# Where the final rows are stored: two output tensors shaped like the result, or one whose rows follow the partitions

## The chip, the cores and the metric

The kernel runs on one core of a Trainium2 chip. The metric is the device time of one launch in microseconds (us). Work that numpy does on the host before or behind the launch is not in it; the joining of output pieces that this case speaks of is such work.

A core has five engines that matter here: PE (matrix products), DVE (element-wise work), ACT (element-wise functions), POOL (small copies and sums) and SP, which computes nothing and issues most of the transfers. A transfer (DMA) is issued by one instruction of SP's queue, and then carried out by the core's 16 DMA engines as packets; here a packet is one run of contiguous bytes, 2 KB in the final stores.

## The reference, cut to what matters

One layer of a streaming encoder is computed for two groups of requests that share the weights: 256 new rows of a prompt and 32 rows of a running sample, each row 2048 numbers wide.

```
xn   = rmsnorm(x, norm_mix_pre);  proj = xn @ w_in
mix  = concat[pool(proj), ssd(proj)] @ w_out
x    = x + rmsnorm(mix, norm_mix_post)
hn   = rmsnorm(x, norm_ffn_pre);  up = conv3(hn @ w_up)
f    = (silu(up[:, :5632]) * up[:, 5632:]) @ w_down
y    = x + rmsnorm(f, norm_ffn_post)      # y_prompt (1, 256, 2048), y_sample (1, 32, 2048)
```

Beside the two `y`, eight histories and states are returned. Everything is float32.

## The kernel before

**Layout.** The 288 rows (256 prompt, 32 sample) stand along the free axis of every tile, and the features along the 128 partitions. A matrix product takes a 128x128 block of a weight and a 128x288 tile of activations. Each float32 operand is split into a rounded part and a rest (`whi`, `wlo`; lines 130 and 131), and each block is multiplied three times (lines 136 to 138). The weights come in by 1 MB transfers that SP issues (`raw`, line 115).

**Order.** A scheduler sets each engine's order from the program, except where the code pins instructions. At the end of the program much is pinned by hand.

**The end of the program.** The down projection gives 16 tiles `part` of 128 features x 288 rows. The result is wanted by rows, so each tile is turned: fourteen of them through DVE's block transpose and a scratch tensor `fd` in DRAM (function `to_tokens`), the last two by PE with an identity (function `turn`). After that a row's features stand along the free axis, in pieces of 512 columns:

- `ft[2*q + b]` is 128 x 512: rows 128*b to 128*b+127 of the prompt, columns 512*q to 512*q+511. There are eight of them, and eight tiles `xr` of the same form, which hold the residual `x`.
- `ft_s` and `xr_s` are 128 x 512 too, but for the sample: with 32 rows only, partition 32*q + s holds row s and columns 512*q to 512*q+511.

What is left is `xr = ft * rf + xr` on DVE (`rf` is the inverse root mean square of each row) and the store. The function `y_out(q, b)` does this for one piece of the prompt and stores it by line 962; the sample's piece is computed in line 1030 and stored by line 1032. The order is: four pieces with b = 1 (their rows are finished first), the sample's piece, then PE's last sums, `rf` for the first 128 rows, and four pieces with b = 0. All nine stores are issued by SP, each 256 KB in 128 runs of 2 KB. Behind them stands the end of the program (line 1105), where SP waits for every DMA semaphore and then all engines meet.

The nine stores in the code:

```python
sp.dma_start(out=y_prompt[0][b * P : (b + 1) * P, 512 * q : 512 * (q + 1)], in_=x)   # line 962, eight times
sp.dma_start(out=y_sample[0].rearrange("s (q c) -> q s c", q=4), in_=xr_s)           # line 1032, once
```

The first store's destination is a pattern of 128 rows x 512 columns with a step of 8 KB from row to row. The second one's is a pattern of three levels: 4 (q) x 32 (s) x 512 (c); q steps by 2 KB and s by 8 KB. On the side of the tile both are 128 partitions x 512 columns.

Of the kernel before, what the change touches and what calls it, by code (L numbers as in the profile page):

```python
# [16 lines left out]
P = 128  # L17
TC = {"schedule_with_timeline_sim": True}
D_MODEL = 2048
NP_ = 256  # L20
NS = 32
NT = NP_ + NS
D_POOL = 1024
D_SSD = 2048
# [6 lines left out]
NF = D_FF // P  # L31
NXC = CONV // P
NU = D_POOL // P
# [10 lines left out]
def body(  # L44
# [14 lines left out]
    w_up2,  # L59
    w_up,  # L60
    w_down,
    y_prompt,
    y_sample,
    new_pool,
    new_sconv,
    new_ssd_p,
# [4 lines left out]
    act, dve, pool, pe, sp = nc.scalar, nc.vector, nc.gpsimd, nc.tensor, nc.sync  # L71
# [97 lines left out]
    def blocks_out(d, t, src, pool_):  # L169
# [17 lines left out]
        out=tri, in_=tri, pattern=[[1, P]], compare_op=ALU.is_ge, fill=0.0, base=0, channel_multiplier=-1  # L187
# [62 lines left out]
    for kb, n in chunks:  # L250
# [12 lines left out]
        for k in range(kb, kb + n):  # L263
# [14 lines left out]
            for m in range(6):  # L278
                c = slice(m * P, (m + 1) * P)
# [75 lines left out]
    def htile(name, n=NT, tag=None):  # L355
        return mp.tile([HEADS, n], F32, tag=tag or name, name=name, bufs={"z": 4}.get(tag, 2) if tag else 1)
# [22 lines left out]
    r = htile("r", tag="z")  # L379
# [295 lines left out]
    for gi in range(2):  # L675
        c = slice(gi * P, (gi + 1) * P)
# [85 lines left out]
    for k in range(KD):  # L762
# [14 lines left out]
        else:  # L777
            q = op_.tile([P, NT], F32, tag="sq", bufs=2, name="sq")
# [11 lines left out]
        for m in range(7):  # L790
            c = slice(m * P, (m + 1) * P)
# [33 lines left out]
    f = []  # L825
# [56 lines left out]
    xr_s = apool.tile([P, 512], F32, tag="a", name="xr_s")  # L882
# [68 lines left out]
    def y_out(q, b):  # L951

        x = xr[2 * q + b]
        f_ = ft[2 * q + b]
        for o, n, src in (
            ((0, 512, f_),) if q < 3 else ((0, 2 * P, f_[:, : 2 * P]), (2 * P, 2 * P, last[b]))
        ):
            c = slice(o, o + n)
            ins = dve.scalar_tensor_tensor(x[:, c], src, rf[:, b : b + 1], x[:, c], op0=ALU.mult, op1=ALU.add)  # L959
            if b:  # L960
                tc.keep_in_program_order(ins)
        sp.dma_start(out=y_prompt[0][b * P : (b + 1) * P, 512 * q : 512 * (q + 1)], in_=x)

    n_tok = [0]

# [20 lines left out]
    for kb, n in ((0, K_RUN), (K_RUN, 8), (K_RUN + 8, 8)):  # L986
# [4 lines left out]
        for piece in split_w(raw, kb, n, 256):  # L991
            for low in (True, False) if kb else (True,):
                for j in range(2):
                    c = slice(j * P, (j + 1) * P)
# [16 lines left out]
    for j in range(2):  # L1011
        c = slice(j * P, (j + 1) * P)
        for i, (k, hi, lo) in enumerate(held):
            tc.keep_in_program_order(
                pe.matmul(pb[j], hi[:, c], f2[k][:, :, B], start=k == K_RUN, stop=k == HALF - 1)
            )
            if j == 0 and i == 13:
                for i in range(2):
                    feature_sums(fsq[i], 0, False, i == 1)
                final_rstd(0)  # L1020
            if j == 1 and i == 2:
                for i in range(2):
                    turn(i, 0)
                act.activation(ft_s[P - NS :, 2 * P :], last[2][P - NS :, :], AF.Copy)
        if j:
            for q in range(4):
                y_out(q, 1)
        run_out(j, 1, pb[j], fsq[j])
    tc.keep_in_program_order(
        dve.scalar_tensor_tensor(xr_s, ft_s, rf[:, 2:3], xr_s, op0=ALU.mult, op1=ALU.add)  # L1030
    )
    sp.dma_start(out=y_sample[0].rearrange("s (q c) -> q s c", q=4), in_=xr_s)
    p_f.append(acc_ps.tile([P, 4], F32, tag="acc", name="psum_f"))
    last[0] = acc_ps.tile([P, 2 * P], F32, tag="acc", name="pft")
    feature_sums(fsum, 1, True, False)
# [5 lines left out]
    for q in range(4):  # L1041
        y_out(q, 0)
# [1 line left out]


_OUTS = [
    (1, 256, 2048), (1, 32, 2048), (P, 2, 15, NU), (P, 2, 3, NXC), (P, D_SSD), (P, D_SSD), (P, 2, 2, 2 * NF),
]


# [70 lines left out]
```

## Time and profile before

| | |
|---|---|
| median of 3 runs | 1338.72 us (1338.0 to 1338.82) |
| the profiled execution's own time | 1337.7 us |
| its span, first to last instruction | 1336.0 us |
| PE busy | 1312.7 us, 98% of the span |
| DVE, ACT, POOL busy | 887.1, 665.3, 239.8 us |
| share of the 16 DMA engines taken by SP's queue | 55.4% |
| moved by DMA | 249.82 MB |

A row of the profile names the line of the code, the engine, the operation and the tiles as out<-in, then count and times. `SPq` is SP's queue: the instruction that issues a transfer, not the transfer itself. In the profile every output tensor is called `out`, so `out<-xr` is one of the eight stores of the prompt's pieces and `out<-xr_s` that of the sample's piece. For transfers a list gives the time from issue to landing, that is, to the semaphore that says that all of it has arrived. In a table by stretches of time, "DMA share" is the mean busy share of the 16 DMA engines, so one engine alone gives 0.06.

### The profile page before, as it was taken

Reading aid. Unit: us, or ns where it says so; the run is one execution under the profiler, and the core shown is the slowest. Engines: PE = TensorE matmul, PEld = TensorE weight load, DVE = VectorE, ACT = ScalarE, POOL = GpSimd, SP = SyncE. Lnnn points to the kernel's source line nnn. Section 1 sums busy time; section 2 is a strip of 40 time slices with the busy share of each in tenths; the row PEclk is TensorE's granted clock in tenths of the full one; section 3 lists DMA queues with packets and bytes.
Section 4 is the critical chain, followed back from the end, with each engine's and each line's share of the span. In section 5 each row is a group of like instructions: output and inputs, shape, how many; then the busy total and the mean of one; then the engine's idle time right before and its main releaser. Section 6 shows DMA issues by size and latency. Waiting matters only on the chain.

```text
span 1336.0 us, 25101 instructions
## 1 busy us (share of the span) xinstructions
PE 1312.7 (98%) x10041; PEld 1297.0 (97%) x10041; DVE 887.1 (66%) x1437; ACT 665.3 (50%) x1002; POOL 239.8 (18%) x376
## 2 busy tenths in 40 slices
PE   7999999999999999999999999999999999999996
PEld 7999999999999989999999999999999999999996
DVE  7898998788544469977676644335666666664444
ACT  7558777446443455644445433334454444454442
POOL 6221102240212123211121100001111111101110
PEclk9999999999999999999999999999999999999998
DMA  7667884456656435766544544554544544566653
GB/s 285 230 194 258 280 248 150 152 207 216 238 205 205 146 121 189 208 180 187 179 158 164 176 146 170 174 182 159 181 166 158 174 174 158 168 239 175 208 177 94
DMA packets 104009, 249.82 MB, mean 187 GB/s; under 512 B 63748, under 2 KB 69444, under 8 KB 81492
## 3 DMA queue, kind: packets, MB, share of 16 engines
q1 hardware_dynamic: 101972, 243.11, 55.4%
q0 software_dynamic: 1488, 4.92, 1.1%
q8 instruction: 78, 1.28, 0.4%
q14 instruction: 39, 0.32, 0.1%
q10 hardware_dynamic: 432, 0.19, 0.1%
HBM read 236.23 MB, written 11.95 MB: 186 GB/s over the span
## 4 chain that ended last, share of the span: by engine, by line
PE 91%; DVE 3%; DMA 2%; issue 1%; POOL 1%; ACT 0%; SPq 0%; DVEq 0%; POOLq 0%; ACTq 0%
PE acc L138 30%; PE acc L136 29%; PE acc L137 29%; DMA xw<-xs_d 1%; POOL xs L640 1%; DMA raw<-in_w_first 1%; DVE xn L100 1%; PE py L467 1%; DMA xs_d<-blocks 1%; DVE wlo L271 0%; DVE xr L959 0%; PE acc_x L138 0%; PE run_a L1002 0%; PE acc_x L137 0%; DVE wlo L131 0%
## 5 line engine op out<-in xcount | busy, mean ns | idle before, releaser
L131 DVE TENSOR_TENSOR wlo<-raw,whi 128x1024 fp32r<-128x1024 f32 (+1 forms) x386 | 464.3, 1204 | 329.4 <-ACT whi L130 328.7
L130 ACT ACTIVATE whi<-raw 128x1024 fp32r<-128x1024 f32 (+1 forms) x386 | 399.3, 1036 | 471.9 <-PE acc L137 384.9
L138 PE MATMUL acc<-hn,wlo 128*128 128x288 f32 x1376 | 409.3, 298 | 0.0
L136 PE MATMUL acc<-hn,whi 128*128 128x288 f32 x1376 | 402.5, 293 | 0.5 <-ACT hn L770 0.5
L137 PE MATMUL acc<-hn,whi 128*128 128x288 f32 x1376 | 399.6, 291 | 1.2 <-DVE hn L771 1.2
L137 PEld LDWEIGHTS acc<-hn,whi 128*128 128x128 f32 x1376 | 258.9, 188 | 1.5 <-DVE hn L771 1.4
L136 PEld LDWEIGHTS acc<-hn,whi 128*128 128x128 f32 x1376 | 258.7, 188 | 1.3 <-ACT hn L770 1.3
L138 PEld LDWEIGHTS acc<-hn,wlo 128*128 128x128 f32 x1376 | 258.7, 188 | 0.0
L136 PE MATMUL acc<-xn,whi 128*128 128x288 f32 x688 | 203.8, 298 | 5.6 <-ACT whi L270 5.6
L137 PE MATMUL acc<-xn,whi 128*128 128x288 f32 x688 | 200.8, 293 | 0.0
L138 PE MATMUL acc<-xn,wlo 128*128 128x288 f32 x688 | 198.7, 298 | 1.6 <-DVE wlo L271 1.4
L138 PE MATMUL acc<-fa,wlo 128*128 128x288 f32 x660 | 196.4, 298 | 0.0
L136 PE MATMUL acc<-fa,whi 128*128 128x288 f32 x660 | 193.1, 293 | 0.0
L137 PE MATMUL acc<-fa,whi 128*128 128x288 f32 x660 | 191.4, 290 | 0.0
L136 PEld LDWEIGHTS acc<-xn,whi 128*128 128x128 f32 x688 | 130.3, 189 | 6.5 <-ACT whi L270 5.6
L137 PEld LDWEIGHTS acc<-xn,whi 128*128 128x128 f32 x688 | 130.3, 189 | 0.2
L138 PEld LDWEIGHTS acc<-xn,wlo 128*128 128x128 f32 x688 | 127.7, 189 | 2.6 <-DVE wlo L271 1.6
L137 PEld LDWEIGHTS acc<-fa,whi 128*128 128x128 f32 x660 | 123.9, 188 | 0.0
L136 PEld LDWEIGHTS acc<-fa,whi 128*128 128x128 f32 x660 | 123.9, 188 | 0.0
L138 PEld LDWEIGHTS acc<-fa,wlo 128*128 128x128 f32 x660 | 123.9, 188 | 0.0
L816 POOL COPY fc_stage<-ebuf 128x4 f32<-128x4 f32 x88 | 27.2, 309 | 466.8 <-DVE ebuf L815 466.8
L812 POOL COPY ebuf<-pf 128x2 f32<-128x2 f32 x88 | 67.4, 767 | 140.6 <-DVE fc L822 79.4
(279 smaller groups left out, 1716.1 us busy)
## 6 DMA issues: line engine op xcount, KB each, us to landing
raw<-in_w_up SPq DMA_DIRECT2D x80, 1024.0 KB, 4.8
raw<-in_w_in SPq DMA_DIRECT2D x38, 1024.0 KB, 5.4
raw<-in_w_down SPq DMA_DIRECT2D x32, 1024.0 KB, 4.8
raw<-in_w_out SPq DMA_DIRECT2D x24, 1024.0 KB, 4.8
raw<-in_w_down SPq DMA_DIRECT2D x16, 768.0 KB, 4.3
raw<-in_w_up SPq DMA_DIRECT2D x8, 896.0 KB, 4.5
gb<-g_d SPq DMA_DIRECT2D x8, 832.0 KB, 6.6
raw<-in_w_first SPq DMA_DIRECT2D x7, 768.0 KB, 10.2
```

What stands on the lines that cost most here:

```text
L100: dve.scalar_tensor_tensor(a[:, 1, :], src, scale, a[:, 0, :].bitcast(F32), op0=ALU.mult, op1=ALU.subtract),
L130: act.activation(hi, raw[:, k : k + n, :], AF.Copy)
L131: dve.tensor_tensor(lo, raw[:, k : k + n, :], hi.bitcast(F32), op=ALU.subtract)
L136: pe.matmul(out, wh, a[:, 0, :], start=start, stop=False)
L137: pe.matmul(out, wh, a[:, 1, :], start=False, stop=False)
L138: pe.matmul(out, wl, a[:, 0, :], start=False, stop=stop)
L467: pe.matmul(y[:, 0:256], xw[:, 0, c], m[:, j, 0:256], start=True, stop=False)
L640: pool.tensor_tensor(xs[t], xs[t], rg[1], op=ALU.mult)
L812: pool.tensor_copy(e[:, 258:260], pf[:, 4:6, i])
L816: pool.tensor_copy(fc_stage[:, :, :, i], e[:, 256:324].rearrange("p (s c) -> p s c", c=34)[:, :, 0:2])
```

## The change

The two output tensors `y_prompt` (1, 256, 2048) and `y_sample` (1, 32, 2048) become one tensor `y_rows` of 128 x 9 x 512. Its first axis is the partition. Piece 4*b + q of the prompt goes to `y_rows[:, 4*b + q, :]` and the sample's piece to `y_rows[:, 8, :]`, exactly as they stand in the tiles. The step from row to row in DRAM is now 9 x 2 KB = 18 KB for all nine stores, and the pattern of each has two levels, 128 x 512. Behind the launch numpy reorders the pieces into the two results.

```diff
-    y_prompt,
-    y_sample,
+    y_rows,
...
-        sp.dma_start(out=y_prompt[0][b * P : (b + 1) * P, 512 * q : 512 * (q + 1)], in_=x)
+        sp.dma_start(out=y_rows[:, 4 * b + q, :], in_=x)
...
-    sp.dma_start(out=y_sample[0].rearrange("s (q c) -> q s c", q=4), in_=xr_s)
+    sp.dma_start(out=y_rows[:, 8, :], in_=xr_s)
...
 _OUTS = [
-    (1, 256, 2048), (1, 32, 2048), (P, 2, 15, NU), (P, 2, 3, NXC), (P, D_SSD), (P, D_SSD), (P, 2, 2, 2 * NF),
+    (P, 9, 512), (P, 2, 15, NU), (P, 2, 3, NXC), (P, D_SSD), (P, D_SSD), (P, 2, 2, 2 * NF),
 ]
...
+    y_p = _np.ascontiguousarray(y[:, :8].reshape(P, 2, D_MODEL).transpose(1, 0, 2)).reshape(1, NP_, D_MODEL)
+    y_s = _np.ascontiguousarray(y[:, 8].reshape(4, NS, 512).transpose(1, 0, 2)).reshape(1, NS, D_MODEL)
```

The end of SP's queue before the change, with what each instruction waits for (a semaphore of DVE, or one of the eight DMA semaphores `DMAHW` that the stores take in turn):

```order
L904 DMA ft_s<-fd 32x256
L962 DMA out<-xr 128x512 [waits DVE_49] x4
L1032 DMA out<-xr_s 4x32x512 [waits DVE_49]
L962 DMA out<-xr 128x512 [waits DMAHW3_49,DVE_49]
L962 DMA out<-xr 128x512 [waits DMAHW4_49,DVE_49]
L962 DMA out<-xr 128x512 [waits DMAHW5_49,DVE_49]
L962 DMA out<-xr 128x512 [waits DMAHW6_49,DVE_49]
L1105 UNCONDITIONAL_BRANCH
```

And the same place of SP's queue after it:

```order
L903 DMA ft_s<-fd 32x256
L961 DMA out<-xr 128x512 [waits DVE_49] x4
L1031 DMA out<-xr_s 128x512 [waits DVE_49]
L961 DMA out<-xr 128x512 [waits DMAHW3_49,DVE_49]
L961 DMA out<-xr 128x512 [waits DMAHW4_49,DVE_49]
L961 DMA out<-xr 128x512 [waits DMAHW5_49,DVE_49]
L961 DMA out<-xr 128x512 [waits DMAHW6_49,DVE_49]
L1104 UNCONDITIONAL_BRANCH
```

Nothing has moved: the lines count one less, the waits are the same, and the one row that reads otherwise is the sample's store, 128x512 in place of 4x32x512. On PE, DVE, ACT and POOL every instruction stands in the same order as before.

More of the change, by code (lines that the diff above doesn't have):

```diff
@@ L1107 @@
     r = _run(nc, [arrays], core_ids=[0])
-    y_p, y_s, n_pool, n_sconv, h_p, h_s, n_fconv = (_np.asarray(r.results[0][f"out_{i}"]) for i in range(len(_OUTS)))
+    y, n_pool, n_sconv, h_p, h_s, n_fconv = (_np.asarray(r.results[0][f"out_{i}"]) for i in range(len(_OUTS)))
     def rows(a, s):
```

## The prediction

> **What bounds the kernel now.** I began with the page's first part and its chain of work, to see whether the end of the program is worth looking at.
>
> ```profile
> span 1336.0 us, 25101 instructions
> PE 1312.7 (98%) x10041; PEld 1297.0 (97%) x10041; DVE 887.1 (66%) x1437; ACT 665.3 (50%) x1002; POOL 239.8 (18%) x376
> ```
>
> PE works for 98% of the span. The change touches none of its instructions and none of its inputs, so what happens before the last product is the same. What counts is how long the core goes on after PE. I read that from the order of time at the end: first DVE and PE's last rows, then SP's queue, both from the view by time.
>
> ```profile
> 1321.85 2.47 DVE L959 SCALAR_TENSOR_TENSOR xr<-ft,rf,xr 128x512 f32<-128x512 f32 x4
> 1324.24 0.48 DVE L959 SCALAR_TENSOR_TENSOR xr<-pft,rf,xr 128x256 f32<-128x256 f32 x1
> 1325.21 0.74 DVE L1030 SCALAR_TENSOR_TENSOR xr_s<-ft_s,rf,xr_s 128x512 f32<-128x512 f32 x1
> 1326.12 0.33 PE L913 MATMUL pft<-ident,part 128*128 128x128 f32 x1
> 1326.60 2.47 DVE L959 SCALAR_TENSOR_TENSOR xr<-ft,rf,xr 128x512 f32<-128x512 f32 x4
> 1328.99 0.48 DVE L959 SCALAR_TENSOR_TENSOR xr<-pft,rf,xr 128x256 f32<-128x256 f32 x1
> ...
> 1322.62 2.45 SPq L962 DMA_DIRECT2D out<-xr  x4
> 1325.98 0.68 SPq L1032 DMA_DIRECT2D out<-xr_s  x1
> 1327.38 4.13 SPq L962 DMA_DIRECT2D out<-xr  x4
> ```
>
> PE is done at 1326.45 us and DVE at 1328.99 + 0.48 = 1329.47. The span ends at 1336.0. So 6.5 us at the end hold no computation at all. The chain of work doesn't show them, since it ends with the last instruction of an engine that computes.
>
> The rows hold a comparison that needs nothing else. The same code runs twice: four pieces with b = 1, and four with b = 0. DVE takes the same time both times (2.47 us and then 0.48 us). SP issues the first four in 2.45 us and the last four in 4.13 us. Between the two stands only the sample's store, whose issue takes 0.68 us. The view of the line of the eight stores gives the range of one issue, and the list of transfers, asked for each piece's stretch of time, the time to landing: first the first piece, then all four of the first group, then the first and the last piece of the second group.
>
> ```profile
> L962 SPq DMA_DIRECT2D out<-xr x8: 332/340/1670, 1322.6 to 1330.3; - x8
> ...
> out<-xr SPq DMA_DIRECT2D x1, 256.0 KB, 2.2
> ...
> out<-xr SPq DMA_DIRECT2D x4, 256.0 KB, 2.1
> ...
> out<-xr SPq DMA_DIRECT2D x1, 256.0 KB, 5.3
> ...
> out<-xr SPq DMA_DIRECT2D x1, 256.0 KB, 4.3
> ```
>
> A piece of the first group lands 2.1 to 2.2 us after its issue, the first of the second group after 5.3 us, and the last one, issued at 1330.3, after 4.3 us: at 1334.6. One issue of the second group takes 1.67 us where the usual one takes 0.34. Something lies in the way of the second group's transfers. The table by stretches of time shows what (us, then busy times of the engines, the PE clock, and last the DMA share and GB/s):
>
> ```profile
> 1323.85:1326.25 2.40, 1.59 (x13) 1.31 (x11) 2.07 (x6) 0.85 (x3) 0.00 (x0) 1.00 0.99 370
> 1327.25:1328.75 1.50, 0.00 (x0) 0.00 (x0) 1.50 (x4) 0.00 (x0) 0.00 (x0) 1.00 0.25 23
> 1328.75:1330.25 1.50, 0.00 (x0) 0.00 (x0) 0.72 (x2) 0.00 (x0) 0.00 (x0) 0.50 0.63 175
> 1330.25:1332.25 2.00, 0.00 (x0) 0.00 (x0) 0.00 (x0) 0.00 (x0) 0.00 (x0) 0.50 0.93 344
> 1332.75:1334.25 1.50, 0.00 (x0) 0.00 (x0) 0.00 (x0) 0.00 (x0) 0.00 (x0) 0.50 0.24 92
> ```
>
> While the first group is moved, the 16 engines are busy for 0.99 of the time at 370 GB/s. The first group's packets begin about 1.2 us behind its first issue (1322.62 to 1323.85); so the sample's store, issued at 1325.98, begins near 1327.25. While it is alone the share is 0.25: four engines of sixteen. And those four move 23 GB/s together, 6 each, where an engine of the first group moves 370 / 16 = 23. At the very end the share is 0.24 again: twelve engines have finished, and the same four still have their part of the last pieces to do, now at full speed (92 / 4 = 23 GB/s each). The waits of SP's queue say it in their way:
>
> ```profile
> SPq L1105 <- DMA out<-xr: 2.4, 4, 0.6
> SPq L1105 <- DMA out<-xr_s: 0.3, 1, 0.3
> L1105 SPq DRAIN x3: 7/7/7, 1334.7 to 1335.0; - x3
> ```
>
> At the end of the program SP waits for the sample's piece (asked by stretches of time, that wait lies between 1331.5 and 1332.1), and then four times 0.6 us for one piece after the other, in a row. About as long does an engine need for its 16 KB of a piece: 256 KB at 370 GB/s is 0.71 us on sixteen engines. Four engines that work off a queue, one piece after another, give just this picture. From the first DRAIN (1334.7) to the end (1336.0) it is another 1.3 us, in which the engines meet.
>
> **The change part by part.**
>
> *The sample's store, 4x32x512 to 128x512.* Before, its 256 KB lie on four engines, 64 KB each. At 23 GB/s an engine that is 2.8 us; it took from 1325.98 to about 1332.1, 6.1 us, since the four hardly moved in their first 1.5 us. The rows of SP's queue behind the change show the same form as for the prompt's pieces, so I take their price: issue 0.34 us in place of 0.68, sixteen engines, 2.0 to 2.2 us to landing, done at about 1328.1. The shorter issue gains nothing by itself: SP's next store waits for DVE and is issued at 1327.38 either way, 0.7 us after the old issue ended.
>
> There is a rule for this in the Trainium skill, "DMA: Bandwidth & Descriptors", section "Why a DMA increments its semaphore by 16 and not by 1": the number of engines is the largest up to 16 that divides the slowest dimension of both patterns, so an outermost 4 gives four engines and 128 gives sixteen. The trace agrees (0.25 of sixteen). By the rule alone, with four engines at their usual pace, the store would have ended at 1327.25 + 2.8 = 1330.1 and the four engines' part of four more pieces at 1332.9, which would leave a gain of 1.4 us; the rows show 1334.6, so 1.6 us belong to the slow start, which the rule doesn't tell of.
>
> *The last four pieces.* With the four engines free, the second group should go like the first. In the first group the issues begin 0.77 us behind DVE's first row (1321.85 to 1322.62) and the last ends at 1322.62 + 2.45 = 1325.07, so the last is issued at 1324.73, 0.01 us after DVE's last part. In the second group the last issue is then at 1329.47 + 0.02 = 1329.49, and it lands 2.0 to 2.2 us later: 1331.5 to 1331.7. Before it landed at 1330.3 + 4.3 = 1334.6. The difference is 2.9 to 3.1 us, and I take 3.0. It consists of the issue, 0.8 us earlier, and of 2.2 us less to landing. The four pieces themselves can't become the bound: one takes 0.71 us on sixteen engines, and they come 0.66 to 0.8 us apart.
>
> *Behind it.* From the last landing the meeting of the engines is what it was, 1.4 us. It is the work that is late next, and the change doesn't touch it.
>
> *The step from row to row, 18 KB in place of 8 KB.* Every packet stays 2 KB, and there are as many. No row shows a store with this step. The nearest are the other stores of 256 KB by 128x512 in SP's queue, at the state's output, where the step is 8 KB:
>
> ```profile
> L707 SPq DMA_DIRECT2D out<-ho x4: 344/404/432, 380.5 to 485.4; - x4
> ...
> DMA to landing us min/median/max: 2.0/2.3/6.7
> ```
>
> They land in 2.0 us at best and 6.7 us at worst, the latter beside weight transfers. I take nothing for the step: 0.99 busy at 370 GB/s in the first group means that the engines themselves set the pace there, and not the place of the bytes. As bounds: no gain, for the same reason; and the worst landing of 6.7 us, put behind the last issue at 1329.49, gives 1336.2 in place of 1334.6, a loss of 1.6 us.
>
> *One output less, two tensors' bytes in one.* Instructions, waits and bytes stay, and the waits of the nine stores are the same, so pieces of one tensor don't wait for each other. What lies outside the span is 1337.7 − 1336.0 = 1.7 us; I take it as unchanged.
>
> **Sum.** Span 1336.0 − 3.0 = 1333.0, and the profiled execution's time 1337.7 − 3.0 = 1334.7. That execution is 1.0 us below the median of the three runs, so against the median 1338.72 I say 1335.7 us. That is 0.22% faster. A measurement of this kernel can tell about 0.2%, 2.7 us, from no change; so even if the mechanism is right, the result may fall within that bound.
>
> **Rivals.**
>
> *The slow start stays.* 23 GB/s on four engines between 1327.25 and 1328.75 has a cause that the views don't name. If it isn't the three-level pattern but the moment or the sample's rows, sixteen engines stand still for 1.6 us in place of four. Then the sample's piece is moved until 1327.25 + 1.6 + 0.7 = 1329.55, and the four behind it follow back to back, 4 x 0.71 = 2.8, until 1332.4; with 0.1 us to landing the gain is 2.1 us, 1336.6 us. Against it: the first piece of the first group meets its tensor for the first time too and lands in 2.2 us, and its issue doesn't stall.
>
> *The wider step makes packets slow; this one ends slower.* It bites on all nine pieces, which then queue on the sixteen engines from the first group on, at 1323.85. The last landing of before, 1334.6, is reached when nine pieces take 10.7 us, 1.2 us a piece in place of 0.71, that is at 0.6 of the first group's speed. Slower by 0.2% needs 2.7 us more, 1.5 us a piece. At 1.6 us a piece the last lands at 1323.85 + 14.4 + 0.1 = 1338.35 and the kernel takes 3.75 us more than before, 1342.5 us. Nothing in the rows speaks for it but that no store with this step is seen.
>
> *The change doesn't do what it says.* If the sample's store still ran on four engines, the time would stay at 1338.7. The two-level form that SP's queue shows after the change, equal to the one that filled sixteen engines, speaks against it.
>
> **How the numbers follow.** The forecast has 0.78, the slow start that stays 0.15, the wider step 0.05 and no effect 0.02. Of the forecast's 0.78 I count 0.66 as measured faster by over 0.2%, since its 2.9 to 3.1 us stand only 0.2 to 0.4 above the bound and the three runs of before lie 0.8 us apart, and 0.12 as within it. With the slow start and no effect, and 0.01 of the step, 0.30 is within 0.2%; 0.04, the rest of the step, is slower. The forecast's own range is 1335.6 to 1335.8 by its terms and 1335.0 to 1336.4 with the spread of the runs. The range for 8 in 10 reaches to the slow start that stays, 1336.6, and as much of the spread above it: 1334.9 to 1337.1.
>
> **What would show it.** In the changed kernel's profile the sample's store should be issued in about 0.34 us and land in 2.0 to 2.2 us; no stretch behind 1327 should show a share of 0.25 at 23 GB/s; the last four stores should be issued within 2.5 us and land in about 2.1 us each; SP's waits for the four pieces at the end should begin near 1330 in place of 1332, with none for the sample's piece; and the span should be near 1333.0 with DVE's end where it was. The prediction is wrong if the DMA share is near 1 at far under 370 GB/s (the step), if all sixteen engines begin slowly (the slow start), or if the end of the program waits for something that these 3 us had hidden.

## The result, and the profile after

The changed kernel took 1333.1 us (median of 6 runs, 1332.54 to 1334.29). Beside them the kernel before had 1337.83 us (6 runs, 1336.96 to 1338.82, of which three are those known ahead of the prediction). The ratio is 0.9968 with a 95% interval of 0.9957 to 0.998, so it is faster by 0.2 to 0.4%. With more runs of both (first experiment below) the ratio is 0.9974 (0.9965 to 0.9983). The forecast was faster by 0.22%, 1335.7 us, in a range of 1334.9 to 1337.1: the direction holds, the time lies 1.8 us below the range.

The page of the changed kernel, and the order of time at its end on DVE and SP:

```profile
span 1332.6 us, 25101 instructions
...
1326.25 2.47 DVE L958 SCALAR_TENSOR_TENSOR xr<-ft,rf,xr 128x512 f32<-128x512 f32 x4
1328.64 0.48 DVE L958 SCALAR_TENSOR_TENSOR xr<-pft,rf,xr 128x256 f32<-128x256 f32 x1
...
1322.27 2.45 SPq L961 DMA_DIRECT2D out<-xr  x4
1325.63 0.33 SPq L1031 DMA_DIRECT2D out<-xr_s  x1
1327.03 2.45 SPq L961 DMA_DIRECT2D out<-xr  x4
```

Now both groups of four are issued in 2.45 us. DVE ends at 1328.64 + 0.48 = 1329.12, and the span 3.5 us later; before, it was 6.5 us. These 3.0 us are the place of the change. The other 0.35 us of the span came before it: DVE's end lay at 1329.47.

The issues of the eight stores in one line, the landing of the sample's store and of the last piece, and the stretches of time that answer to those shown of before:

```profile
L961 SPq DMA_DIRECT2D out<-xr x8: 332/332/345, 1322.3 to 1329.1; - x8
...
out<-xr_s SPq DMA_DIRECT2D x1, 256.0 KB, 2.0
...
out<-xr SPq DMA_DIRECT2D x1, 256.0 KB, 2.0
```

```profile
1323.50:1325.90 2.40, 1.59 (x13) 1.31 (x11) 2.07 (x6) 0.85 (x3) 0.00 (x0) 1.00 1.00 372
1326.90:1327.60 0.70, 0.00 (x0) 0.00 (x0) 0.70 (x3) 0.00 (x0) 0.00 (x0) 1.00 0.37 138
1328.00:1330.00 2.00, 0.00 (x0) 0.00 (x0) 1.12 (x3) 0.00 (x0) 0.00 (x0) 0.50 0.99 371
```

No issue takes longer than 0.35 us (before: up to 1.67). Each store lands in 2.0 to 2.1 us. The second group goes at 371 GB/s, the first at 372. The sample's piece is a short burst in between, from 1326.46 to 1327.3 us. The second stretch holds the end of it: 0.37 of the time at 138 GB/s, 23 GB/s for each engine that works (138 / (0.37 x 16)), where before it was four engines with 6 GB/s each. SP's waits at the end:

```profile
SPq L1104 <- DMA out<-xr: 1.3, 2, 0.7
L1104 SPq DRAIN  x3: 7/7/7, 1331.3 to 1331.6; - x3
```

The wait for the sample's piece is gone, and the last piece has landed by 1331.3 in place of 1334.7. From there to the end it is 1.3 us as before.

### The profile page after: what moved, and what is told of

Read it like the earlier page. It is cut to its first block, busy times and chain, and to the rows that moved or that the text cites. A ratio compares the mean times of both kernels' runs of the same rounds, so it can differ in the third digit from the quotient of the medians.

```text
span 1332.6 us, 25101 instructions
## 1 busy us (share of the span) xinstructions
PE 1312.0 (98%) x10041; PEld 1296.3 (97%) x10041; DVE 887.4 (67%) x1437; ACT 666.0 (50%) x1002; POOL 241.5 (18%) x376
## 4 chain that ended last, share of the span: by engine, by line
PE 94%; DVE 4%; DMA 1%; issue 1%; ACT 0%; POOL 0%; DVEq 0%; SPq 0%; POOLq 0%; ACTq 0%
PE acc L137 31%; PE acc L135 29%; PE acc L136 29%; PE py L466 1%; DVE wlo L788 1%; DVE hn L770 0%; DVE xn L99 0%; DVE mg L757 0%; DVE wlo L130 0%; DVE xr L958 0%; PE run_a L1001 0%; DVE win L609 0%; DMA raw<-in_w_in 0%; PE low L999 0%; DMA raw<-in_w_first 0%
```

## The experiments

Two questions were open. Does the whole gain come from the sample's store, and is it 3 us or the 4.7 us of the first difference of medians? And what makes four engines start at 6 GB/s each? Beside the timed ratio I use one number of the profile, the time from the end of DVE's last instruction to the end of the span ("the tail"). What varies from execution to execution ahead of that point isn't in it. It repeats well: 3.5 us in three executions whose sample's store is 128x512, 6.5 to 6.6 us in three with four engines on that store ahead of the last pieces. From the fifth experiment on there is one profiled execution of each kernel and the tail alone is read. The times of these six are, in the order below, 1337.80, 1336.73, 1334.93, 1335.09, 1334.62 and 1335.94 us. The kernel before took 1338.04 us beside the first four and 1335.73 beside the last two, so single times tell nothing of the change. Transfers on fewer than sixteen engines have no time to landing in the list; for these it is read from the steps of their semaphore in the trace.

**The changed kernel again.** No edit, more runs.

> The changed kernel once more, to settle the size. Theory of the four engines: the end of the program is 3.0 to 3.1 us shorter, nothing else, so the ratio is 0.9977 with the difference of the medians 2.5 to 3.6 us, and the larger difference seen first (4.7 us) was scatter between executions. Rival, that something outside the last 15 us gained too: the ratio stays at 0.9965 to 0.997, over 4 us.

Measured: 1334.2 us (11 runs, 1332.57 to 1334.87) against 1337.42 (33 runs of before, 1335.55 to 1339.91): 3.2 us between the medians, ratio 0.9974 (0.9965 to 0.9983). The page's first line and DVE's last row in the order of time:

```profile
span 1332.0 us, 25101 instructions
1328.05 0.48 DVE L958 SCALAR_TENSOR_TENSOR xr<-pft,rf,xr 128x256 f32<-128x256 f32 x1
```

The tail is 1332.0 − 1328.53 = 3.5 us again. The gain is that of the tail; what the first difference, 4.7 us, had beyond it was scatter. The 33 runs of before lie 4.4 us apart, where the three known at first lay within 0.8.

**The sample's store alone.** The prompt's output stays as it was.

```diff
-    sp.dma_start(out=y_sample[0].rearrange("s (q c) -> q s c", q=4), in_=xr_s)
+    sp.dma_start(out=y_sample, in_=xr_s)
...
-    (1, 256, 2048), (1, 32, 2048), (P, 2, 15, NU), ...
+    (1, 256, 2048), (P, 512), (P, 2, 15, NU), ...
```

> Only the sample's store goes to a 128x512 output of its own; the prompt's pieces are stored as before (step 8 KB, two output tensors). Theory of the four engines: the whole gain, 2.5 to 3.6 us, the sample's store issued in 0.33 us and landing in 2.0 us, the last piece landing 2.1 us after its issue. Rival, that the 18 KB step or the single tensor brings a part: the gain is at least 1 us smaller than that of the whole change.

Measured: 1334.27 us, ratio 0.9979 (0.997 to 0.9988). DVE's last row and SP's rows in the order of time, under the page's first line:

```profile
span 1331.4 us, 25101 instructions
1327.42 0.48 DVE L959 SCALAR_TENSOR_TENSOR xr<-pft,rf,xr 128x256 f32<-128x256 f32 x1
1324.41 0.33 SPq L1032 DMA_DIRECT2D out<-xr_s  x1
1325.81 2.45 SPq L962 DMA_DIRECT2D out<-xr  x4
```

The tail is 1331.4 − 1327.90 = 3.5 us: the whole gain with one of the nine stores changed, and with two outputs and the 8 KB step kept for the other eight.

**The prompt's stores alone.**

```diff
-        sp.dma_start(out=y_prompt[0][b * P : (b + 1) * P, 512 * q : 512 * (q + 1)], in_=x)
+        sp.dma_start(out=y_prompt[:, 4 * b + q, :], in_=x)
...
-    (1, 256, 2048), (1, 32, 2048), (P, 2, 15, NU), ...
+    (P, 8, 512), (1, 32, 2048), (P, 2, 15, NU), ...
```

> Only the prompt's pieces go to a 128x8x512 output (step 16 KB); the sample's store stays 4x32x512. Theory of the four engines: no gain, within 0.7 us of before; the store of the sample takes 0.68 us to issue, a stretch with DMA share 0.25 stays, and the last piece lands 4 to 5 us after its issue. Rival, that the rows' step brings a part: at least 1 us faster.

Measured: 1337.37 us, ratio 1.0001 (0.9992 to 1.001). DVE's last row and SP's rows in the order of time:

```profile
1330.06 0.48 DVE L959 SCALAR_TENSOR_TENSOR xr<-pft,rf,xr 128x256 f32<-128x256 f32 x1
...
1327.05 0.70 SPq L1032 DMA_DIRECT2D out<-xr_s  x1
1328.44 4.12 SPq L962 DMA_DIRECT2D out<-xr  x4
```

The stretch in which the sample's store is alone, by the table of stretches:

```profile
1328.30:1329.80 1.50, 0.00 (x0) 0.00 (x0) 1.50 (x4) 0.00 (x0) 0.00 (x0) 0.50 0.24 22
```

The span is 1337.1 us, the tail 1337.1 − 1330.54 = 6.6 us, and everything of before is there again: the issue of 0.70 us, the share of a quarter at 22 GB/s, 4.12 us for the last four issues. A step of 16 KB in place of 8 KB brings nothing that can be seen.

**Four stores in place of one, to the same places as before.**

```diff
-    sp.dma_start(out=y_sample[0].rearrange("s (q c) -> q s c", q=4), in_=xr_s)
+    for q in range(4):
+        sp.dma_start(out=y_sample[0][:, 512 * q : 512 * (q + 1)], in_=xr_s[NS * q : NS * (q + 1), :])
```

> Both outputs as before; the sample's piece is stored by four stores of 32x512, one for each q, to the same places. Theory of the four engines: 32 rows go to all sixteen engines, so the time is that of the changed kernel within 0.7 us though the destination and its 8 KB step are as before; SP's four issues of 0.35 to 0.43 us end near 1327.4 to 1327.7, 0 to 0.3 us behind the time at which the next piece is ready, which later pieces make up. Rival, that the place of the sample's rows in DRAM makes the slow start: the stores still begin slowly, share well under 0.9 for 1 us or more, and the gain is 2.1 us or less.

Measured: 1335.22 us, ratio 0.9986 (0.9977 to 0.9995). DVE's last row and SP's rows in the order of time, under the page's first line:

```profile
span 1333.0 us, 25104 instructions
1328.28 0.48 DVE L959 SCALAR_TENSOR_TENSOR xr<-pft,rf,xr 128x256 f32<-128x256 f32 x1
1325.28 1.76 SPq L1033 DMA_DIRECT2D out<-xr_s  x4
1327.14 1.98 SPq L962 DMA_DIRECT2D out<-xr  x4
```

and the table by stretches of time:

```profile
1326.40:1328.30 1.90, 0.00 (x0) 0.00 (x0) 1.90 (x5) 0.00 (x0) 0.00 (x0) 0.54 0.56 163
```

The tail is 1333.0 − 1328.76 = 4.2 us: 2.3 of the 3.0 us, without any change of the outputs. It misses the changed kernel by 0.75 us, a little more than expected. The trace shows two parts: SP's four issues last until 1327.04, the pieces behind them are issued closer together, and the last one lands 2.5 us after its issue in place of 2.0; and since three transfers more have shifted the turn of the DMA semaphores, the last piece's semaphore stands early in SP's list of waits at the end, and six waits of 0.06 us follow on its landing. The share of 0.56 looks like the rival's sign, but 64 KB are 0.18 us of work for sixteen engines at 370 GB/s, and SP issues them 0.39 to 0.47 us apart. What tells is the pace of an engine that works, 163 / (0.56 x 16) = 18 GB/s, three times what it was at the same places.

**Where does the slow start come from? Four engines, other places.** The sample's store goes to `y_sample[:, :32, :]` of a 4x33x512 output, so that it keeps its three levels, but each engine writes 64 KB that lie together.

```diff
-    sp.dma_start(out=y_sample[0].rearrange("s (q c) -> q s c", q=4), in_=xr_s)
+    sp.dma_start(out=y_sample[:, :32, :], in_=xr_s)
...
-    (1, 256, 2048), (1, 32, 2048), (P, 2, 15, NU), ...
+    (1, 256, 2048), (4, 33, 512), (P, 2, 15, NU), ...
```

> As before, but the sample's store goes to an output of its own of 4x33x512, of which 4x32x512 are written: still three levels with an outer 4, still four engines, but each engine's 32 runs of 2 KB now lie one behind the other in DRAM. What is compared is the time from DVE's last instruction to the end of the span: 6.5 us before, 3.5 us changed. If the slow start of the four engines (1.6 us at 6 GB/s each) belongs to the pattern or to the use of four engines: 6.5 us, with a stretch of share 0.25 at some 23 GB/s. If it belongs to the place of the runs in DRAM (step 8 KB, four engines writing neighbouring 2 KB): 4.9 us, with 90 GB/s at share 0.25.

The page's first line and DVE's last row in the order of time:

```profile
span 1336.1 us, 25101 instructions
1329.10 0.48 DVE L959 SCALAR_TENSOR_TENSOR xr<-pft,rf,xr 128x256 f32<-128x256 f32 x1
```

and the table by stretches of time:

```profile
1327.36:1328.86 1.50, 0.00 (x0) 0.00 (x0) 1.50 (x4) 0.00 (x0) 0.00 (x0) 0.63 0.25 23
1332.86:1334.36 1.50, 0.00 (x0) 0.00 (x0) 0.00 (x0) 0.00 (x0) 0.00 (x0) 0.50 0.24 92
```

The same 23 GB/s at a share of 0.25, and a tail of 1336.1 − 1329.58 = 6.5 us. The place in DRAM isn't it.

**The sample's store last.** The edit moves line 1032 behind the four pieces with b = 0 and pins the order of these five stores.

```diff
-        sp.dma_start(out=y_prompt[0][b * P : (b + 1) * P, 512 * q : 512 * (q + 1)], in_=x)
+        ins = sp.dma_start(out=y_prompt[0][b * P : (b + 1) * P, 512 * q : 512 * (q + 1)], in_=x)
+        if not b:
+            tc.keep_in_program_order(ins)
...
-    sp.dma_start(out=y_sample[0].rearrange("s (q c) -> q s c", q=4), in_=xr_s)
...
     for q in range(4):
         y_out(q, 0)
+    tc.keep_in_program_order(
+        sp.dma_start(out=y_sample[0].rearrange("s (q c) -> q s c", q=4), in_=xr_s)
+    )
```

> As before, but the sample's store is issued behind the last prompt piece, so that nothing queues behind it. The last prompt piece should then land 2.0 to 2.2 us after its issue, as in the changed kernel. The sample's store, issued some 0.4 us behind DVE's end, lands 6.0 us later if it starts slowly by itself (7.8 us from DVE's end to the end of the span, some 1.3 us slower than before), or 4.2 us later if the slow start needs the issues that come behind it (6.0 us).

DVE's last row and SP's rows in the order of time, under the page's first line:

```profile
span 1335.0 us, 25100 instructions
1326.63 0.48 DVE L959 SCALAR_TENSOR_TENSOR xr<-pft,rf,xr 128x256 f32<-128x256 f32 x1
1327.53 0.70 SPq L1045 DMA_DIRECT2D out<-xr_s  x1
```

and the table by stretches of time:

```profile
1329.20:1330.30 1.10, 0.00 (x0) 0.00 (x0) 0.00 (x0) 0.00 (x0) 0.00 (x0) 0.50 0.19 11
1331.30:1333.00 1.70, 0.00 (x0) 0.00 (x0) 0.00 (x0) 0.00 (x0) 0.00 (x0) 0.50 0.24 94
```

The tail is 1335.0 − 1327.11 = 7.9 us, as expected for a slow start of its own. With nothing queued behind it, the store still moves only 11 GB/s in the stretch from 1329.2 to 1330.3, 1.7 us and more after its issue, and then 94 GB/s, the full pace of four engines. Its semaphore shows it landed at 1333.6, 6.1 us after its issue. The last piece of the prompt, ahead of it, lands in 2.0 us.

**Sixteen engines, three levels.** As with the padded output, but 16x9x512, of which 16x8x512 are written.

```diff
-    sp.dma_start(out=y_sample[0].rearrange("s (q c) -> q s c", q=4), in_=xr_s)
+    sp.dma_start(out=y_sample[:, :8, :], in_=xr_s)
...
-    (1, 256, 2048), (1, 32, 2048), (P, 2, 15, NU), ...
+    (1, 256, 2048), (16, 9, 512), (P, 2, 15, NU), ...
```

> As before, but the sample's store goes to an output of 16x9x512, of which 16x8x512 are written: three levels as before, but the outer dimension is 16, so sixteen engines. If four engines are what costs: 3.5 us from DVE's end to the end of the span, as in the changed kernel, landing in 2.0 to 2.4 us, even if the issue takes 0.7 us. If the three levels make the slow start whatever the number of engines: the sixteen stand still for some 1.6 us and it is 4.4 us or more.

DVE's last row and SP's rows in the order of time, under the page's first line:

```profile
span 1333.2 us, 25101 instructions
1329.01 0.48 DVE L959 SCALAR_TENSOR_TENSOR xr<-pft,rf,xr 128x256 f32<-128x256 f32 x1
1326.00 0.66 SPq L1032 DMA_DIRECT2D out<-xr_s  x1
```

and the table by stretches of time:

```profile
1327.25:1328.00 0.75, 0.00 (x0) 0.00 (x0) 0.75 (x3) 0.00 (x0) 0.00 (x0) 0.54 0.85 177
```

The tail is 1333.2 − 1329.49 = 3.7 us. Almost all is gained, but not quite: the engines work for 0.85 of the first 0.75 us and move 177 GB/s, half their pace, and the store lands 3.0 us after its issue, not 2.0 to 2.4. Three levels have a price of their own even on sixteen engines; the issue of 0.66 us is part of it, the slower start the rest.

**Four engines, two levels.** Rows 0 to 115 in one store, rows 116 to 127 in another; and then the first of these alone, a kernel that leaves the last twelve rows out and serves for the trace only.

```diff
-    sp.dma_start(out=y_sample[0].rearrange("s (q c) -> q s c", q=4), in_=xr_s)
+    sp.dma_start(out=y_sample[:116], in_=xr_s[:116])
+    sp.dma_start(out=y_sample[116:], in_=xr_s[116:])
...
-    (1, 256, 2048), (1, 32, 2048), (P, 2, 15, NU), ...
+    (1, 256, 2048), (P, 512), (P, 2, 15, NU), ...
```

> The sample's piece goes to a 128x512 output by two stores of two levels: rows 0 to 115, whose 116 divides by 4 but by no larger number up to 16, and rows 116 to 127. If the store of 116 rows runs on four engines, a stretch with share 0.25 shows with two levels only. If the slow start belongs to four engines with about 30 runs each: 6.0 to 6.5 us from DVE's end to the end of the span and some 23 GB/s in that stretch. If it belongs to the three levels: about 4.6 to 4.9 us and 80 to 92 GB/s. If the number of engines doesn't follow the outer dimension, it is 3.5 us and no stretch of 0.25.

> The store of rows 0 to 115 of the sample's piece alone, two levels, four engines with 29 runs each; the other twelve rows are left out. If two levels have a slow start of their own on four engines: first 0.5 to 1.5 us at share 0.25 and under 60 GB/s, landing 4.5 to 5.0 us after the issue, 5.0 to 5.4 us from DVE's end to the end of the span. If the slow start seen with two stores was made by the store of the last twelve rows: share 0.25 at 80 to 92 GB/s from the beginning, landing at 3.9 us, and 4.4 to 4.8 us to the end.

With both stores the tail is 1333.4 − 1328.04 = 5.4 us, between the two expectations; the two stores overlap in time, so it can't be read further. The second kernel, with the first store alone: its page's first line, DVE's last row and the issue of the store,

```profile
span 1332.9 us, 25101 instructions
1327.21 0.48 DVE L959 SCALAR_TENSOR_TENSOR xr<-pft,rf,xr 128x256 f32<-128x256 f32 x1
1324.20 0.33 SPq L1032 DMA_DIRECT2D out<-xr_s  x1
```

and the table by stretches of time:

```profile
1325.00:1326.75 1.75, 0.00 (x0) 0.00 (x0) 1.75 (x3) 0.00 (x0) 0.00 (x0) 0.68 0.29 57
1330.25:1331.00 0.75, 0.00 (x0) 0.00 (x0) 0.00 (x0) 0.00 (x0) 0.00 (x0) 0.50 0.23 87
```

The share of about a quarter says four engines (0.29 with the first packets of the next piece in the stretch; up to 1326.40, ahead of them, it is 0.26 at 51 GB/s), with two levels only and with 116 rows outermost. They too start slowly (57 GB/s for 1.75 us, 87 at the end). The store lands 4.7 us after its issue and the tail is 1332.9 − 1327.69 = 5.2 us. The issue of 0.33 us is that of any two-level store; but behind it, two of the four next issues took 0.83 and 0.71 us.

**Eight engines, three levels.** 8x17x512, of which 8x16x512 are written.

```diff
-    sp.dma_start(out=y_sample[0].rearrange("s (q c) -> q s c", q=4), in_=xr_s)
+    sp.dma_start(out=y_sample[:, :16, :], in_=xr_s)
...
-    (1, 256, 2048), (1, 32, 2048), (P, 2, 15, NU), ...
+    (1, 256, 2048), (8, 17, 512), (P, 2, 15, NU), ...
```

> The sample's store goes to an output of 8x17x512, of which 8x16x512 are written: three levels, outer 8. Theory: the outer dimension sets the number of engines, and the slow start grows as fewer engines are used: a stretch with share 0.5, the store lands 3.5 to 4.5 us after its issue (6.0 with an outer 4, 3.0 with an outer 16), and from DVE's end to the end of the span it is 4.3 to 5.1 us (6.5 and 3.7). Rival, that only an outer 4 is bad: as with 16, below 3.9 us.

The page's first line and DVE's last row in the order of time:

```profile
span 1334.2 us, 25101 instructions
1328.67 0.48 DVE L959 SCALAR_TENSOR_TENSOR xr<-pft,rf,xr 128x256 f32<-128x256 f32 x1
```

and the table by stretches of time:

```profile
1327.00:1328.25 1.25, 0.00 (x0) 0.00 (x0) 1.25 (x3) 0.00 (x0) 0.00 (x0) 0.50 0.48 64
```

Half the engines, 64 GB/s, landing 4.4 us after the issue, a tail of 1334.2 − 1329.15 = 5.05 us: as expected, at the upper end.

**Together.** In the changed kernel a piece lands 2.0 to 2.1 us after its issue, of which its moving takes 0.71 us (eight runs of 2 KB on each engine, 0.09 us a run). So by these stores full pace is 1.35 us, and 0.09 us for each run of an engine. What a store took beyond that:

| the sample's store | runs an engine | at full pace | landed after | beyond | tail |
|---|---|---|---|---|---|
| 128x512, sixteen engines (changed) | 8 | 2.1 | 2.0 | 0 | 3.5 |
| 16x8x512, sixteen engines | 8 | 2.1 | 3.0 | 0.9 | 3.7 |
| 8x16x512, eight engines | 16 | 2.8 | 4.4 | 1.6 | 5.05 |
| 116x512, four engines | 29 | 4.0 | 4.7 | 0.7 | 5.2 |
| 4x32x512, four engines (before) | 32 | 4.2 | 6.1 | 1.9 | 6.5 |

Both count: few engines, and three levels. Neither alone makes the whole slow start.

The trace of before also says where in the store it lies. Here are the DMA share in forty slices of 1322 to 1325 us (the first group) and of 1327 to 1328 us (the sample's store), as tenths, and the packets of 1327 to 1328, 1328 to 1328.5, 1328.5 to 1329 and 1329 to 1329.5 us:

```profile
DMA  0000000000000000000499979999999999999999
...
DMA  0000000000025008303000399000900000000000
...
DMA packets 12, 0.02 MB, mean 25 GB/s; under 512 B 0, under 2 KB 0, under 8 KB 12
...
DMA packets 3, 0.01 MB, mean 12 GB/s; under 512 B 0, under 2 KB 0, under 8 KB 3
...
DMA packets 9, 0.02 MB, mean 37 GB/s; under 512 B 0, under 2 KB 0, under 8 KB 9
...
DMA packets 22, 0.05 MB, mean 90 GB/s; under 512 B 0, under 2 KB 0, under 8 KB 22
```

The first group's packets begin at 1323.45, 0.8 us behind its first issue, the sample's at 1327.28, 1.3 us behind its own. The other traces agree: 0.8 us with two levels (128x512 and 116x512), 1.3 to 1.4 us with three (outermost 4, 8 and 16). So of what a three-level store takes beyond full pace, 0.5 us passes ahead of its first packet. The rest, 0.4, 1.1 and 1.4 us with sixteen, eight and four engines (0.7 us for four engines with two levels), lies in slow packets: in before the eight packets that start between 1327.58 and 1328.53 take 0.35 to 0.92 us each, where one usually takes 0.08 to 0.09.

And it isn't only the four engines that are slow. The first piece of the second group is issued at 1327.38, so its packets on the twelve other engines were due at 1328.2. But all engines together move 37 GB/s from 1328.5 to 1329 and 90 from 1329 to 1329.5, no more than four engines at full pace. So the twelve start about 1 us late, although the four alone finish last.

What makes the packets slow wasn't found. The place in DRAM and what is queued behind are excluded, each by one execution. Which partitions of the tile an engine reads was not varied by itself: with fewer engines, each reads more of them. So this stays open.

## Why the prediction was right in its mechanism and wrong in its time

- *Four engines of sixteen carry the sample's store, and the pieces behind it wait for them.* Right: the sample's store alone gives the whole gain (tail 3.5 us), the prompt's stores alone none (6.6 us). The twelve other engines start late too, which the prediction didn't see; the four still set the end.
- *The end is 2.9 to 3.1 us shorter.* Right: 6.5 to 3.5 us in the tail, and 3.2 us between the medians of 11 and 33 runs. The sample's store was issued in 0.33 us and landed in 2.0, the last piece too. Both parts are there: the last issue comes 0.03 us behind DVE's end in place of 0.83, and its landing 2.0 us later in place of 4.3.
- *The step from row to row costs nothing.* Right within 0.1%: 1.0001 (0.9992 to 1.001) with 16 KB, and the 18 KB of the changed kernel show 371 to 372 GB/s. The reason given was weak, though: a share of 0.99 need not mean that the engines set the pace, since in the slow start four engines counted as busy all the time at a quarter of theirs.
- *The slow start that stays.* It didn't. The prediction left open what it belongs to; the runs put it with the use of few engines and the three levels.
- *Sixteen engines for 128x512, four for 4x32x512*, by the rule of the Trainium skill, "DMA: Bandwidth & Descriptors", section "Why a DMA increments its semaphore by 16 and not by 1": the shares of 0.25, 0.48, 0.85 and 0.29 with outer sizes of 4, 8, 16 and 116 agree with it. The steps of the stores' semaphores count the engines more directly: four, eight, sixteen and four steps that come with the data. That with four engines at full pace only 1.4 us were to be gained is a sum that no run here tests; the 1.6 us that it puts down to the slow start lie near the 1.9 us that the store took beyond full pace.
- *"The first group's packets begin about 1.2 us behind its first issue."* A misreading: they begin 0.8 us behind it, and 1323.85 is only where the stretch in the table starts. That the sample's store begins near 1327.25 is right by luck, since three levels take 1.3 us. The 3.0 us don't rest on it; they come from landing times.
- *The predicted time and its range failed.* The step that failed is in the sum, from 1334.7 us (the profiled execution less 3.0) to 1335.7, and the range "with the spread of the runs" around it. I took the three runs' median, 1338.72, as the level and their 0.8 us as the scatter. More runs put the level at 1337.83 (6 runs) and 1337.42 (33 runs), with 4.4 us between the lowest and the highest. Of the 2.6 us between 1335.7 and 1333.1, 0.9 us is the level, and 1.7 us the difference of 4.7 us in those six runs against 3.0, which the larger sample took back to 3.2. With a level of 1337.42 the same sum gives 1334.4; the changed kernel's 11 runs have 1334.2.

The traces show where the scatter arises. In the profiles shown DVE's last instruction ends between 1327.1 and 1330.5 us, in kernels whose work is the same up to there, so it lies ahead of the place of the change. The store of `fc_stage`, some 145 us before DVE's end, already has it: here in before, in the changed kernel again, and with the prompt's stores alone.

```profile
L870 SPq DMA_DIRECT2D out<-fc_stage x1: 360/360/360, 1184.3 to 1184.3; - x1
...
L869 SPq DMA_DIRECT2D out<-fc_stage x1: 360/360/360, 1183.3 to 1183.3; - x1
...
L870 SPq DMA_DIRECT2D out<-fc_stage x1: 360/360/360, 1185.3 to 1185.3; - x1
```

DVE's end follows 145.2 us behind in all three. Matched one by one, the products of PE between 536 and 1318 us keep their distances to 0.01 us in all twelve traces. All of the scatter between these executions arises in the first 536 us; from what there wasn't followed up.

## What to carry to other kernels

When a kernel's last work is a row of stores, compare groups of equal stores with each other: if one lands in 2 us and the next in 5, look at the store between them, and at the DMA share while it is alone; a quarter or a half says how many engines it runs on. Write a store so that its outermost size on both sides fills the sixteen engines and that it has two levels, and let the host or the layout of the output take up the reordering; where the output can't change, several stores of 32 rows did most of it here (2.3 of 3.0 us). And for a gain of some tenths of a per cent, three runs tell neither the level nor the scatter; a stretch of the profile that begins just ahead of the change (here the tail) repeated within 0.1 us while whole times lay 4.4 us apart.

## What the runs showed of the hardware that I had not expected

A store on few engines doesn't run at its share of the bandwidth: four engines moved 23 GB/s together in their first 1.5 us, then 92. Three levels alone cost a store on sixteen engines about 1 us to landing (3.0 in place of 2.0), half of it ahead of the first packet, and 0.33 us at issue (0.66 in place of 0.33). And a store that is itself on sixteen engines pays in its issue for one ahead of it on four: the queue of SP stood for 1.67 us in one issue before, and for 0.83 us behind the store of 116 rows.
